# A two-layer decoder trunk on one core: the second layer in a hand-written TensorE order

## The chip, the cores and the metric

The kernel runs on one NeuronCore of one Trainium2 chip. The metric is the device time in microseconds of one execution. Engines go by the profile's names: PE (TensorE matmul), PEld (its weight loads), DVE (VectorE), ACT (ScalarE), POOL (GpSimd), SP (the queue that issues the DMAs).

## The reference

The input is 2048 tokens of width 1024. Layer 1 is gated linear attention, layer 2 dilated sliding-window attention in three (window, dilation) groups; each layer also has a small cross-attention into 256 memory tokens, a SiLU gate and an output projection. Layer 2, which the change concerns:

```
def dilated_mixer(h, w_in):
    for g, (window, dil) in enumerate(DIL_GROUPS):     # (128, 1), (512, 4), (2048, 16)
        qkv = (h @ w_in[:, base:base + 3 * 768]).reshape(B, T, 3, 6 heads, 128)
        q, k = partial_rope(qkv[:, :, 0]), partial_rope(qkv[:, :, 1])      # 32 of 128 dims turn
        o, lse = dilated_group(q, k, qkv[:, :, 2], window, dil)
    wts = softmax over the 3 groups of lse
    o = sum over groups of wts * outs
    ...                                                # q_mem and gate from the last columns
branch = concatenate([mix, mem_o]) * silu(gate)
x = x + branch @ w_out[i]
return rmsnorm(x, final_norm_w)
```

All of it is float32; the kernel splits each operand into a high and a low part and multiplies high by high, high by low and low by high.

## The kernel before, in words

**Helpers.** `mm3` (L178) is those three matmuls, at lines 179, 180 and 181, so nearly all TensorE work stands under three lines and is told apart by its tiles. `split_P` (L169) makes high (L172, ACT) and low (L173, POOL) halves of a probability tile and transposes both with one DMA (L174). `load_w` (L128) loads a block of weight columns, takes its norm (two squares on ACT, L114; a matmul with ones over the partitions, L118; a scale that is a power of two) and splits it (L138, L139). `mm_bank` (L730) hands out three PSUM banks in turn: two of `ps_mm`, one of `ps_x`. Scores use the two banks of `ps_g`, the value products the one bank of `ps_o`.

**Order.** The framework plans the order on every engine from an estimate of each instruction's time; PE too follows that plan. Every engine runs its own list in order.

**Layer 1** (up to about 932 us) ends with `a2_h2`, which writes `h2T`, the normed input of layer 2, transposed, in high and low halves (f16).

**Strassen stage** (L751 to L955). Thirteen sets of 256 columns of `w_in_b` (one of memory queries; three of gates, the gate of heads 4 and 5 not among them; nine of v, one for each pair of heads and each group) are multiplied by a one-level Strassen scheme: `sums` (L763) makes S1, S2 and S4 from quarters of `h2T` and overwrites one quarter with S3; `load_ws` (L788) makes seven combinations of a set's weights; `sblock` (L819) does seven products of 12 matmuls for half of the tokens, evacuated at L835, L840 and L842. Results go to DRAM: v transposed (`out_v`, `v_d`), gates after SiLU (`out_gate`, `sg_d`), queries (`qm_d`). Beside it runs the memory attention, one block of 128 tokens a step: `mem_a` (scores, softmax, transposing DMA) and, one step later, `mem_b` (values). At the end the overwritten quarter of `h2T` is loaded again from `a21_d`.

**Heads** (L957 to L1180). Nine units (pair of heads, group), two heads each. `proj_qk` (L985) makes q and k of one head, for four chunks of 512 tokens each: 24 matmuls, then the rope on that one tile: a shuffle (L1002, DVE), a product with the sines (L1003, POOL), one with the cosines (L1004, DVE, on the PSUM tile), their sum (L1005, DVE), and the high (L1007, ACT) and low (L1008, DVE) halves, which free the bank. `attend` (L1012) takes sixteen blocks of 128 queries two at a time: scores, mask and maximum (L1037), exponentials (L1048), `split_P`, value products, copy out (L1067, to `o_d`). `gate_prep` (L1086) and `gate_item` (L1121) later mix the three groups by their softmax weights (`fb`, read back from DRAM to all partitions) and multiply by the gate, into `br_d`; POOL has two of the products (L1135, L1140). Those of the first two pairs of heads run among later units; the last pair's stand after all heads, with the gate projection `gate_mm` of heads 4 and 5.

**Projection** (L1205 on). For sixteen blocks of 128 tokens `load_b` (L1209) loads and splits the branch (L1216, L1217); 2 x 24 matmuls of 512 columns in f32 parts follow (256-wide pieces in half of the last block), then the residual (L1244), the norm and the store.

Of the kernel before, what the change touches and what calls it, by code (L numbers as in the profile page):

```python
# [34 lines left out]
def trunk(ctx, tc, a, out):  # L35
# [259 lines left out]
    def silu(ps, n, inv, neg, dst, wk):  # L295
        e = tl(wk, [P, 512], F32, "e")
# [28 lines left out]
    v_d = {(hp, g, i): tl(dram, [P, 2, NB, P], F16, f"vd{hp}_{g}_{i}") for hp in range(3) for g in range(3)  # L325
           for i in range(2)}
    sg_d = {h: tl(dram, [P, T], F32, f"sgd{h}") for h in (0, 1, 2, 3, 6, 7)}
# [399 lines left out]

# [8 lines left out]

    def gdst(t, g, c):
# [7 lines left out]
    wp = c3.enter_context(pool("wpb", 4))  # L745
# [4 lines left out]

    with ExitStack() as cv:  # L751
        c4p = cv.enter_context(pool("c4p", 5))
        uv = cv.enter_context(pool("uv", 2))
        svp = cv.enter_context(pool("svp", 1))
        mc = cv.enter_context(pool("mc", 1))
        mk = cv.enter_context(pool("mk", 1))
        H = T // 2
        Ss = {n: tl(svp, [P, 2, 4, H], F16, n) for n in ("S1", "S2", "S4")}

# [3 lines left out]
        def sums(ts):  # L763
            n = ts.stop - ts.start

            def f32(i, k, eng):
                t = tl(c4p, [P, 4, n], F32, "c4")
                eng.tensor_tensor(out=t, in0=quad(i, k, 0, ts), in1=quad(i, k, 1, ts), op=ALU.add)
                return t

            def split(t, hi, lo, eng):
                A.activation(out=hi, in_=t, func=AF.Copy)
                eng.tensor_tensor(out=lo, in0=t, in1=hi, op=ALU.subtract)

            s = f32(1, 1, V)
            x21 = f32(1, 0, G)
            V.tensor_tensor(out=s, in0=s, in1=x21, op=ALU.add)
            split(s, Ss["S1"][:, 0, :, ts], Ss["S1"][:, 1, :, ts], V)
            x11 = f32(0, 0, G)
            V.tensor_tensor(out=s, in0=s, in1=x11, op=ALU.subtract)  # L780
            split(s, Ss["S2"][:, 0, :, ts], Ss["S2"][:, 1, :, ts], V)
            G.tensor_tensor(out=x21, in0=x11, in1=x21, op=ALU.subtract)
            split(x21, quad(1, 0, 0, ts), quad(1, 0, 1, ts), G)
            x12 = f32(0, 1, G)
            V.tensor_tensor(out=s, in0=x12, in1=s, op=ALU.subtract)
            split(s, Ss["S4"][:, 0, :, ts], Ss["S4"][:, 1, :, ts], V)

        def load_ws(c0, cps):  # L788
# [4 lines left out]
            wa = tl(wp, [P, 4, 2, 4, P], F16, "w")  # L793
            wb = tl(wp, [P, 3, 2, 4, P], F16, "w")
            junk = wa.rearrange("p f a k n -> p (f a k n)").bitcast(BF16)
            s, inv = norm_scale(raw, [junk[:, i * 1024:(i + 1) * 1024].rearrange("p (k n) -> p k n", n=256)
                                      for i in range(2)], cps)
            t13 = tl(c4p, [P, 2, 4, P], F32, "c4")
            t24 = tl(c4p, [P, 2, 4, P], F32, "c4")
            rq = raw.rearrange("p (q k) n -> p q k n", q=2)  # L800
            top = raw[:, 0:4, :].rearrange("p k (q n) -> p q k n", q=2)
            low = raw[:, 4:8, :].rearrange("p k (q n) -> p q k n", q=2)
            G.tensor_tensor(out=t13, in0=rq[:, :, :, P:2 * P], in1=top, op=ALU.subtract)
            G.tensor_tensor(out=t24[:, 0], in0=low[:, 1], in1=t13[:, 0], op=ALU.subtract)
            G.tensor_tensor(out=t24[:, 1], in0=low[:, 0], in1=t24[:, 0], op=ALU.subtract)
            A.activation(out=wb[:, 2, 0], in_=top[:, 0], func=AF.Copy, scale=s)
            A.activation(out=wa[:, 0:2, 0], in_=low, func=AF.Copy, scale=s)
            A.activation(out=wa[:, 2:4, 0], in_=t13, func=AF.Copy, scale=s)
            A.activation(out=wb[:, 0:2, 0], in_=t24, func=AF.Copy, scale=s)
            for src, dst in ((top[:, 0], wb[:, 2]), (low[:, 0], wa[:, 0]), (low[:, 1], wa[:, 1]),  # L810
                             (t13[:, 0], wa[:, 2]), (t13[:, 1], wa[:, 3]), (t24[:, 0], wb[:, 0]),
                             (t24[:, 1], wb[:, 1])):
                V.scalar_tensor_tensor(out=dst[:, 1], in0=src, scalar=s, in1=dst[:, 0], op0=ALU.mult,
                                       op1=ALU.subtract)
            V.tensor_tensor(out=inv, in0=inv, in1=invh1, op=ALU.mult)
            return dict(B21=wa[:, 0], B22=wa[:, 1], T1=wa[:, 2], T3=wa[:, 3], T2=wb[:, 0], T4=wb[:, 1],
                        B11=wb[:, 2]), inv

        def sblock(w, cc, sc):  # L819
            ts = slice(cc * 512, (cc + 1) * 512)  # L820
            aform = {"A11": quad(0, 0, 0, ts), "A12": quad(0, 1, 0, ts), "A22": quad(1, 1, 0, ts),
                     "S3": quad(1, 0, 0, ts)}
# [486 lines left out]
```

## Time and profile before

| | us |
|---|---|
| runs (median of 3; lowest, highest) | 2785.2; 2782.36, 2786.55 |
| the profiled execution: its time; its span | 2786.99; 2785.2 |
| busy in it: PE, PEld, DVE, ACT, POOL | 2553.5, 1679.4, 1697.5, 1205.8, 735.5 |
| mean granted TensorE clock | 0.967 |

The span runs from the first to the last instruction. A matmul's duration in the profile takes in its way through the array, so neighbours overlap and the busy share of PE reads high; the pace is read from one start to the next. The granted clock is 1 or 0.5 of full speed from moment to moment, and a window shows its mean.

### The profile page before, as it was taken

How to read it: one execution, taken by the hardware profiler on the slowest of the kernel's cores; microseconds unless marked ns; L12 is line 12 of the kernel's file. 1: busy time of each engine (PE TensorE's matmuls, PEld its weight loads, DVE VectorE, ACT ScalarE, POOL GpSimd, SP SyncE). 2: the span in 40 equal slices, each digit the busy share in tenths (PEclk: the TensorE clock that was granted, in tenths of full speed). 3: DMA queues.
4: the chain of work that ended last, by engine and by line, in shares of the span. 5: the costliest groups of instructions: out<-in, count | busy, mean ns of one | idle time of the engine just before them, and what ended most of it. 6: DMA issues, size and time to landing. Idle time of an engine off the chain costs nothing. (4 is left out here: it accounts for less than half of the span.)

```text
span 2785.2 us, 44184 instructions
## 1 busy us (share of the span) xinstructions
PE 2553.5 (92%) x16725; PEld 1679.4 (60%) x16725; DVE 1697.5 (61%) x3514; ACT 1205.8 (43%) x2635; POOL 735.5 (26%) x550
## 2 busy tenths in 40 slices
PE   7989999999998679989889999998899988996899
PEld 6879998888987334444444455554455544553677
DVE  6345444655566876455545767768777688765543
ACT  6356444544344355444445344434344333434122
POOL 0000000100002554334442233334543345331200
PEclk9999999999999789999999999999999999997899
DMA  6242113343333125576764434336843377425643
GB/s 205 85 137 72 58 53 113 103 101 88 97 103 92 55 67 140 126 160 138 162 144 107 150 85 99 98 82 168 215 134 91 83 197 199 107 77 144 220 161 118
DMA packets 522297, 336.62 MB, mean 121 GB/s; under 512 B 373170, under 2 KB 475236, under 8 KB 519780
## 3 DMA queue, kind: packets, MB, share of 16 engines
q1 hardware_dynamic: 522084, 333.80, 44.1%
q8 instruction: 131, 2.15, 0.3%
q14 instruction: 82, 0.67, 0.1%
HBM read 178.99 MB, written 89.57 MB: 96 GB/s over the span
## 5 line engine op out<-in xcount | busy, mean ns | idle before, releaser
L179 PE MATMUL ps_mm<-h2T,w 128*128 128x512 f16 x1128 | 435.5, 386 | 29.3 <-ACT c L840 12.7
L181 PE MATMUL ps_mm<-h2T,w 128*128 128x512 f16 x1128 | 435.2, 386 | 0.0
L180 PE MATMUL ps_mm<-h2T,w 128*128 128x512 f16 x1128 | 435.1, 386 | 0.0
L179 PE MATMUL ps_mm<-w,hT 128*128 128x256 f16 (+1 forms) x1408 | 388.3, 276 | 3.9 <-ACT v L488 1.9
L180 PE MATMUL ps_mm<-w,hT 128*128 128x256 f16 (+1 forms) x1408 | 387.1, 276 | 0.0
L181 PE MATMUL ps_mm<-w,hT 128*128 128x256 f16 (+1 forms) x1408 | 385.7, 275 | 0.4 <-DVE hT L382 0.4
L180 PEld LDWEIGHTS <-w 128*128 128x128 f16 x1944 | 192.3, 99 | 251.3 <-issue 55.0
L181 PEld LDWEIGHTS <-w 128*128 128x128 f16 x1944 | 192.6, 99 | 223.8 <-issue 21.3
L179 PEld LDWEIGHTS <-w 128*128 128x128 f16 x1944 | 192.7, 99 | 221.9 <-issue 16.6
L1003 POOL TENSOR_TENSOR sh<-sh,rope 32x512 f32<-32x512 f32 x144 | 183.7, 1276 | 328.4 <-DVE sh L1002 309.1
L173 POOL TENSOR_TENSOR stg<-mp,stg 128x512 f16<-128x512 f32 x16 | 18.6, 1161 | 838.9 <-DMA ogd<-og 460.2
L1048 ACT ACTIVATE pm<-pm,st,cols 128x256 f32<-128x256 f32 (+1 forms) x288 | 156.3, 544 | 189.5 <-DVE st L1042 187.0
L173 POOL TENSOR_TENSOR ph<-pm,ph 128x512 f16<-128x512 f32 (+2 forms) x144 | 139.6, 976 | 263.0 <-issue 144.4
L179 PE MATMUL ps_x<-h2T,w 128*128 128x512 f16 x504 | 192.2, 381 | 0.4 <-ACT c L842 0.4
L181 PE MATMUL ps_x<-h2T,w 128*128 128x512 f16 x504 | 192.5, 382 | 0.0
L180 PE MATMUL ps_x<-h2T,w 128*128 128x512 f16 x504 | 192.4, 382 | 0.0
L179 PEld LDWEIGHTS <-hT 128*128 128x128 f16 x1408 | 139.1, 99 | 24.4 <-issue 5.4
L180 PEld LDWEIGHTS <-hT 128*128 128x128 f16 x1408 | 139.0, 99 | 23.7 <-issue 5.3
L181 PEld LDWEIGHTS <-hT 128*128 128x128 f16 x1408 | 139.5, 99 | 18.2 <-DVE hT L382 0.7
L114 ACT ACTIVATE w<-stg 128x1024 bf16<-128x1024 f32 (+1 forms) x78 | 82.0, 1051 | 113.5 <-DMA stg<-in_w_in_b 70.2
L859 ACT ACTIVATE vh<-c 128x1024 f16<-128x1024 f32 x36 | 60.4, 1678 | 131.7 <-DMA vo<-vh 78.5
L179 PE MATMUL ps_g<-k,q 128*128 128x256 f16 (+1 forms) x288 | 70.2, 251 | 31.0 <-DVE mx L1037 26.6
(353 smaller groups left out, 5941.2 us busy)
## 6 DMA issues: line engine op xcount, KB each, us to landing
stg<-in_w_in_b SPq DMA_DIRECT2D x64, 512.0 KB
v<-vd SPq DMA_DIRECT2D x18, 1024.0 KB
od<-osb SPq DMA_DIRECT2D x72, 256.0 KB
og<-od SPq DMA_DIRECT2D x72, 256.0 KB
fb<-fd SPq DMA_DIRECT2D x24, 768.0 KB
x<-in_x SPq DMA_DIRECT2D x32, 512.0 KB
vd<-vo SPq DMA_DIRECT2D x48, 256.0 KB
hTd<-hT SPq DMA_DIRECT2D x16, 512.0 KB
```

The lines of the kernel that those rows point to most:

```text
L114: A.activation(out=junk[i], in_=hv, func=AF.Square, accum_out=rm[:, i:i + 1])
L173: G.tensor_tensor(out=lo, in0=src, in1=hi, op=ALU.subtract)
L179: PE.matmul(o, sh, mh, start=first, stop=False)
L180: PE.matmul(o, sh, ml, start=False, stop=False)
L181: PE.matmul(o, sl, mh, start=False, stop=last)
L859: A.activation(out=hi, in_=src, func=AF.Copy)
L1003: G.tensor_tensor(out=sw, in0=sw, in1=rs, op=ALU.mult)
L1048: A.activation(out=p_, in_=p_, func=AF.Exp, scale=sc, bias=st[:, j:j + 1], accum_out=st[:, 16 + j:17 + j])
```

## The change

Only layer 2 changes. PE follows the order in which the program is written (`manual_schedule` for PE alone); the other engines are planned as before.

- *Strassen stage.* The memory queries (192 matmuls) and the gate of head 4 (96) are done first, by ordinary projections, chunk by chunk, while `sums`, now in eight parts, are made. Twelve sets stay. Between the products of a block `side(i)` puts the next set's norm, combinations and splits, the memory attention (`mem_b` of one block after product 4, `mem_a` of the next after product 5) and what is left of the sums. `v_d` is laid out in chunks of whole rows.
- *Heads.* One head after another, each with groups 16, 4, 1. A stage is one chunk of q or of k (24 matmuls); stage s also holds the scores of step s − 10 and the value products of step s − 13, ahead of its projection. The rope is done for a chunk's q and k together after the second of them, with their 32 turning rows stacked in one tile. A head's weights are loaded, normed and split among the stages of the head before. The mixing is done per head, its loads some stages ahead of its products.
- *End.* The gate of head 5 is projected in eight halves beside the last head's scores and value products; that head's last group stays in SBUF (`osb`), as does its finished branch (`b5s`). `w_out` is split before. The projection takes the other seven 128-row blocks of the branch first (`f_main`) and head 5's last (`f_fin`); three such parts stand before the last value products are done. The first 512 output columns are done as two 256-wide pieces, for the weights lie in separate tiles.

```
+    def proj_t(w, c):
+        t = mm_bank()
+        for k in range(KT):
+            mm3(t, w[:, 0, k], w[:, 1, k], h2T[:, 0, k, cs], h2T[:, 1, k, cs], k == 0, k == KT - 1)
+        return t
...
+        cv.enter_context(tc.manual_schedule(engines={mybir.EngineType.PE}))
...
+        def sums(x):
+            ts = slice(x * P, (x + 1) * P)
+            x21 = f32q(1, 0, ts, G)
+            s = f32q(1, 1, ts, V)
+            V.tensor_tensor(out=s, in0=s, in1=x21, op=ALU.add)
+            split(s, Ss["S1"][:, 0, :, ts], Ss["S1"][:, 1, :, ts], V)
...
+        memq(2)
+        out_q(0, 0, proj_t(wq["w"][0], 0))
+        pair_norm(wg4, ps_g)
+        pair_split(wg4, 0)
...
+        out_q(0, 1, proj_t(wq["w"][1], 0))
+        gate4(2)
+        sums(0)
+        sums(1)
+        gate4(0)
+        sums(2)
+        memq(1)
+        set_norm(cur, ps_g)
+        sums(3)
...
+    def rope_pair(ts, c, g, dsts):
+        r0 = 64 * (c // 2)
+        rt = [rope[x][r0:r0 + 64, (c % 2) * 512:(c % 2 + 1) * 512] for x in range(2)]
+        X = tl(bk, [P, 512], F32, "rx")[r0:r0 + 64, :]
+        W = tl(bk, [P, 512], F32, "rw")[r0:r0 + 64, :]
+        for j in range(2):
+            A.activation(out=X[32 * j:32 * j + 32, :], in_=ts[j][0:32, :], func=AF.Copy)
+        V.stream_shuffle(W, X, SWAP)
+        G.tensor_tensor(out=W, in0=W, in1=rt[1], op=ALU.mult)
+        V.tensor_tensor(out=X, in0=X, in1=rt[0], op=ALU.mult)
+        for j in range(2):
+            V.tensor_tensor(out=ts[j][0:32, :], in0=X[32 * j:32 * j + 32, :], in1=W[32 * j:32 * j + 32, :], op=ALU.add)
+        for j in range(2):
+            hi = gdst(dsts[j][:, 0, :], g, c)
+            A.activation(out=hi, in_=perm(ts[j], g), func=AF.Copy, scale=SQ)
+            V.scalar_tensor_tensor(out=gdst(dsts[j][:, 1, :], g, c), in0=perm(ts[j], g), scalar=SQ, in1=hi,
+                                   op0=ALU.mult, op1=ALU.subtract)
...
+    for s in range(NS):                       # 18 heads x 8 stages
+        n, e = divmod(s, 8)
+        if s >= 10:
+            scores(s - 10)
+        if s >= 13:
+            pv(s - 13)
...
+        live[e % 2] = proj_t(d["w"][e % 2], e // 2)
+        if e % 2 == 1:
+            rope_pair([live[0], live[1]], e // 2, u[1], hds[n]["qk"])
+            wcur = wnext
+        if e == 2:
+            pair_norm(wcur, ps_tr)
+        elif 4 <= e < 4 + wcur["m"]:
+            pair_split(wcur, e - 4)
+        if e == 6:
+            hds[n]["v"] = load_v(n)
+        h, x = divmod(s - 35, 24)
+        if 0 <= h < 5:
+            step = 4 if h < 4 else 2
...
+            y, z = divmod(x - 5, step)
+            if 0 <= y < 4 and z == 0:
+                item_mix(*items.pop(y))
+            y, z = divmod(x - 3, step)
+            if 0 <= y < 4 and z == 0:
+                items[y] = (item_og(h, y), item_fb(h, y))
...
+    for x in range(14):
+        if x < 10:
+            scores(NS - 10 + x)
+        if x < 13:
+            pv(NS - 13 + x)
...
+        if x < 8:
+            gate_half(x)
...
+            P1, P2 = [(0, 256), (256, 256)], [(512, 512)]
...
+        if x in (8, 9):
+            fs[x - 8] = load_b(x - 8)
...
+        if x == 9:
+            f_main(fs[0], P1)
+        if x == 10:
+            f_main(fs[1], P1)
+        if x == 12:
+            f_main(fs[0], P2)
+            fs[2] = load_b(2)
```

More of the change, by code (lines that the diff above doesn't have):

```diff
@@ L807, in load_ws @@
[L807 to L814, printed above, removed]
@@ new lines, in trunk @@
+        out_q(0, 1, proj_t(wq["w"][1], 0))
[7 more added lines that the diff above has]
+        sums(3)
+        for x in ("T1", "T2", "T3", "T4"):
+            set_diff(cur, x)
+        gate4(1)
+        sums(4)
+        for x in range(4):
+            set_split(cur)
+        memq(3)
+        sums(5)
+        gate4(3)
+        for x in range(3):
+            set_split(cur)
+        late = [lambda x=x: sums(x) for x in (6, 7)]
```

931 lines of the change are left out of this document (545 added, 386 removed).

## The prediction

> **What bounds the kernel now.** I read the page's busy shares and clock row first, then windows cut at the program's stages, then PE's waits in each window, then the timeline for the pace of one matmul.
>
> ```profile
> PE 2553.5 (92%) x16725; PEld 1679.4 (60%) x16725; DVE 1697.5 (61%) x3514; ACT 1205.8 (43%) x2635; POOL 735.5 (26%) x550
> PEclk9999999999999789999999999999999999997899
> ```
>
> TensorE is busy for 92% of the span, no other engine for more than 61%; its clock row dips at the start of layer 2 and at its end. The columns of the windows are length, PE, PEld, DVE, ACT, POOL busy, granted clock, DMA share, GB/s:
>
> ```profile
> 0.00:886.00 886.00, 847.89 (x7441) 758.60 (x7442) 474.46 (x1094) 429.69 (x1003) 41.06 (x52) 0.99 0.33 100
> 886.00:932.00 46.00, 27.14 (x190) 21.20 (x188) 36.57 (x48) 18.28 (x34) 21.48 (x10) 0.78 0.33 104
> 932.00:1010.00 78.00, 45.52 (x162) 18.64 (x162) 70.93 (x48) 28.68 (x37) 58.16 (x23) 0.73 0.13 38
> 1010.00:1540.00 530.00, 486.25 (x2469) 229.01 (x2467) 282.88 (x441) 256.26 (x411) 205.10 (x130) 0.97 0.59 140
> 1540.00:2515.00 975.00, 924.43 (x5493) 484.33 (x5492) 708.07 (x1714) 394.67 (x978) 373.12 (x314) 0.99 0.49 125
> 2515.00:2612.00 97.00, 61.04 (x287) 37.28 (x283) 50.69 (x81) 35.88 (x69) 19.72 (x15) 0.79 0.60 181
> 2612.00:2779.00 167.00, 161.27 (x696) 130.39 (x696) 71.92 (x88) 41.35 (x100) 16.90 (x8) 0.96 0.46 157
> 2779.00:2785.20 6.20, 0.00 (x0) 0.00 (x0) 1.96 (x4) 1.00 (x4) 0.00 (x0) 0.78 0.23 85
> ```
>
> Row 1 is layer 1, unchanged. The others are: layer 1's last block, the start of layer 2, the Strassen products, the attention heads, gates and last combinations, the output projection, and the tail. PE stands idle there for 46 − 27.1 = 18.9, 32.5, 43.8, 50.6, 36.0 and 5.7 us, 187 us in all. While busy it also loses (1 − clock) × busy: 6 + 12.3 + 14.6 + 9.2 + 12.8 + 6.5 = 61 us. About 249 us of layer 2 are thus not matmul work at full pace, and only these can be won. Who ended the idle time, window by window:
>
> ```profile
> PE ps_g L118 <- DVE rb L116: 6.8, 1, 6.8
> PE ps_tr L166 <- DVE sg L692: 6.1, 1, 6.1
> ...
> PE ps_mm L179 <- ACT c L840: 10.0, 2, 6.5
> PE ps_g L258 <- DMA qmT<-qmd: 9.0, 1, 9.0
> ...
> PE ps_mm L179 <- DVE uv L835: 11.6, 3, 6.1
> PE ps_o L284 <- DMA mp<-mh: 11.4, 6, 5.3
> ...
> PE ps_g L179 <- DVE mx L1037: 23.3, 21, 3.6
> PE ps_o L179 <- DMA pt<-ph: 13.2, 18, 2.2
> ...
> PE ps_x L179 <- POOL fb L1135: 20.0, 1, 20.0
> PE ps_o L179 <- DMA pt<-ph: 6.1, 6, 2.2
> ```
>
> Nearly all are waits for a result that was asked for too soon: a score bank whose maximum isn't taken (L1037), probabilities not yet transposed (pt, mp), a combination not yet made. No engine is full, except VectorE in 932 to 1010 (70.9 of 78 us).
>
> **The change part by part.** The pace of matmuls, from starts (the first two pairs stand ten steps apart, the last pair are neighbours):
>
> ```profile
> 1603.09 0.38 PE L180 MATMUL ps_mm<-h2T,w 128*128 128x512 f16 x1
> ...
> 1605.25 0.38 PE L181 MATMUL ps_mm<-h2T,w 128*128 128x512 f16 x1
> ...
> 2759.67 0.39 PE L179 MATMUL ps_mm<-wh,w 128*128 128x512 f32 x1
> ...
> 2761.94 0.39 PE L180 MATMUL ps_mm<-wl,w 128*128 128x512 f32 x1
> ...
> 2775.41 0.28 PE L181 MATMUL ps_mm<-wh,w 128*128 128x256 f32 x1
> 2775.53 0.28 PE L179 MATMUL ps_mm<-wh,w 128*128 128x256 f32 x1
> ```
>
> A 512-wide f16 step is 2.16 / 10 = 0.216 us, an f32 one 2.27 / 10 = 0.227, a 256-wide f32 one 0.12.
>
> *Added matmuls.* The memory queries leave the Strassen form: 8 x 24 = 192 matmuls for 14 products x 12 = 168, so 24 x 0.216 = +5.2 us. The first half of the output columns is done in 256-wide pieces, for 16 blocks: 16 x 24 x (2 x 0.12 − 0.227) = +5.0 us. Gates of heads 4 and 5 keep their 192 matmuls and move. Together +10 us, all on PE's path.
>
> *Start (886 to 1010).* The 192 query matmuls and 96 of gate 4, 62 us at pace, now stand ahead of the first Strassen product and need only h2T and their weights. The cover for them is VectorE's: it must meanwhile make the sums 0 to 3 (eight 128x512 steps each). The nearest row, of twice the size:
>
> ```profile
> L773 DVE TENSOR_TENSOR S<-c,S x12: 1212/1944/3361, 934.9 to 1006.1; 128x1024 f16<-128x1024 f32 x12
> ```
>
> Half its median is 0.97: 4 x 8 x 0.97 = 31 us; sixteen query splits and eight gate steps at about 0.7 us (L1005's row, below) add 17, seven weight splits of the sums' size 7, three of twice that 6: 61 of 62 us. By the row's ends the sums alone are 20 or 54 us, so nothing or some 25 us stay uncovered; the row's smallest value is what an undisturbed step takes, and I take a value between, near the covered end: of 32.5 idle us I keep 6. Gate 4 brings per chunk 24 matmuls, two VectorE and three ACT steps and one store on SP, none of which anything waits for before the items. Layer 1's last block still ends in the same chain (rb, sg above): of 18.9 I keep 15 (bounds 5 and 25).
>
> *Strassen products.* Each memory PV now follows its scores by seven products (7 x 12 x 0.216 = 18 us) where the mp transposes made PE wait. Weight splits go two to a product, operand by operand; what is late next is the product's own evacuation (L835, three banks). Of 43.8 I keep 14 (bounds 3 and 44). The stores of v become whole 2 KB rows, the weight loads of the heads 512-byte rows; at a DMA share of 0.59 and 0.49 I cost both at nothing: they have a set or a head's eight stages (50 us) of cover. SP issues in order, so a late transpose holds up those loads; without cover each would cost its lateness.
>
> *Heads.* Scores now lag projections by ten stages, PV lags scores by three. The scores and PV of 144 stages are three lines each of these (the wide ones 0.108 us, half a 512 step, the narrow ones 0.054):
>
> ```profile
> L179 PE MATMUL ps_g<-k,q 128*128 128x256 f16 x162 | 44.3, 275 | 23.8 <-DVE mx L1037 19.6 <-ACT k L1007 3.6
> L179 PE MATMUL ps_g<-k,q 128*128 128x128 f16 x126 | 26.2, 220 | 7.2 <-DVE mx L1037 7.0
> L179 PE MATMUL ps_o<-pt,v 128*128 128x128 f16 x318 | 60.8, 221 | 21.7 <-DMA pt<-ph 19.3 <-DVE osb L1067 2.0
> L179 PE MATMUL ps_o<-pt,v 128*128 128x256 f16 x66 | 18.0, 273 | 0.0
> ```
>
> That is 3 x (228 x 0.108 + 444 x 0.054) / 144 = 1.0 us a stage beside 24 x 0.216 = 5.2 us of projection, so PV has 18 us of cover: the 23.3 and 13.2 us of waits above go. New is the pairing of q's and k's rope.
>
> ```profile
> L1002 DVE STREAM_SHUFFLE sh<-ps_mm x96: 715/723/746, 1541.1 to 2490.4; 32x512 f32<-32x512 f32 x96
> L1003 POOL TENSOR_TENSOR sh<-sh,rope x144: 1252/1262/1775, 1544.7 to 2498.0; 32x512 f32<-32x512 f32 x144
> L1004 DVE TENSOR_TENSOR ps_mm<-ps_mm,rope x96: 676/685/693, 1544.5 to 2491.2; 32x512 f32<-32x512 f32 x96
> L1005 DVE TENSOR_TENSOR ps_mm<-ps_mm,sh x96: 685/687/687, 1546.1 to 2492.6; 32x512 f32<-32x512 f32 x96
> L1007 ACT ACTIVATE q<-ps_mm x48: 569/588/597, 1548.2 to 2475.1; 128x512 f16<-128x512 f32 x48
> L1008 DVE SCALAR_TENSOR_TENSOR q<-ps_mm,q x48: 615/691/693, 1549.7 to 2476.4; 128x512 f16<-128x512 f32 x48
> ```
>
> Each of 72 pairs saves a shuffle and a cosine product (72 x 1.41 = 101 us of VectorE's 708), a GpSimd product (91 us of 373), and adds two ACT copies (at most L1007's 0.59 each: 85 us on 395). None of the three was the bound, so this gives PE nothing by itself. But q's bank is now held through k's projection. After that projection ends the chain is 0.59 (copy) + 0.72 + 1.26 + 2 x 0.69 (adds) + 0.69 (low part) = 4.6 us; the bank is wanted 5.2 + 2 x 1.0 = 7.2 us after, so 2.6 us are left for queueing. How long such queues get:
>
> ```profile
> ACT k L1007 <- DVE ps_mm L1005: 119.6, 31, 7.8
> POOL fb L1135 <- DMA fb<-fd: 27.0, 8, 5.7
> L1144 DVE TENSOR_TENSOR fb<-fb x24: 677/692/1641, 1921.0 to 2662.4; 128x512 f32<-128x512 f32 x24
> ```
>
> 31 waits of ACT for VectorE's rope add sum to 119.6 us, one of 7.8: most pairs fit, some don't. At 0.25 us a pair this is 18 us; with 12 us of other waits I keep 30 of 50.6 (bounds 8, and 72 x 1.4 = 101). Twenty gate items are spread at four stages each with fb loaded two stages (12 us) ahead; the four of head 4 come into the heads: six DMAs each on SP, whose two-stage lead covers them, and about 3.5 us each on VectorE and GpSimd, hidden while VectorE is at (708 − 101 + 14) / 955 = 65%. Without that cover they cost 4 x 3.5 = 14 us.
>
> *End.* The 20.0 us wait for the last items goes: 96 gate matmuls (20.7 us) now run beside the last scores and PV, head 5 skips its o and br round trips, and three parts of the projection start on seven blocks. New: the first branch load needs h2T's space, freed by the last gate matmul; load, copy and subtract (some 3 to 8 us) meet only four score and PV groups, 2.6 us. Of 36.0 I keep 9 (bounds 4 and 25). *Projection:* 3 of 5.7 stay; the tail of 6.2 us stays.
>
> **Sum.** Idle kept: 15 + 6 + 14 + 30 + 9 + 3 = 77, so 110 us go. Half-rate loss shrinks in the same proportion, 61 to 25: 36 us go. 110 + 36 − 10 = 136. The profiled execution took 2787.0 us, 1.8 more than its span of 2785.2, which is also the runs' median; 2785 − 136 gives about 2648 for the median.
>
> **A rule against it.** VectorE's L1004 reads one operand from PSUM and stays within 0.693 us beside GpSimd; L1144 reads two from SBUF and reaches 1.641. In the new rope the cosine product reads X and the table, both SBUF, just as GpSimd multiplies W. If one stands still for the other, each chain grows by 0.69 to 5.3 us. The Trainium skill, SBUF — State Buffer, section Who interferes with whom, says that a VectorE instruction with two SBUF inputs contends with a GpSimd instruction that reads SBUF, one waiting for the whole of the other; L1144's spread agrees. By that rule the sum would be 50 us higher if no slack were left, unchanged if 2 us remain.
>
> **Rivals.**
> - *Every gap goes* (lags of three to ten stages cover all queues): keeps 5 + 2 + 3 + 8 + 4 + 2 = 24, loss 8: 163 + 53 − 10 = 206, 2579 us. Against: the 7.8 us queue.
> - *The rope holds the banks:* each pair late by 0.69 us more, 72 x 0.69 = 50: 2698 us. For it: L1144; against: 101 us less VectorE work.
> - *The fixed order does nothing in the middle* (products and heads keep their idle time): the start and end alone give 29 + 27 + 3 and some 20 of clock, less 10: 2716 us.
> - *Slower than before:* GpSimd stands in order at an item's fb, and behind it the rope and the splitting of probabilities, so PE stops. Twenty items must each lose 136 / 20 = 6.8 us. With two stages, 12.4 us, of lead fb would have to land after 19 us; its longest overhang here was 5.7. Then 2785 or more.
>
> **How the numbers follow.** My forecast 0.55 (its own range 2605 to 2690), every gap 0.15, rope 0.18, middle unchanged 0.05, slower 0.07. The range 2590 to 2735 leaves out half of "every gap" and all of "slower", under 2 in 10. A measurement here tells 0.2% (5.6 us) from no change: faster 0.91, same 0.02, slower 0.07.
>
> **What would show it.** Right: heads' window near 925 us with clock 0.99 or more; no wait of PE for L1037's maximum or pt; the start without a dip to 0.73; no 20 us wait after the gates; 256-wide f32 steps of 0.12. Wrong: PE waiting every second stage for the low part of q, or for rb of a weight norm; GpSimd idle on fb for over 6 us; VectorE above 90% in the heads.

## The result, and the profile after

The changed kernel takes 2749.4 us (median of 4 runs, 2743.2 to 2756.2), the kernel before 2785.9: a ratio of 0.9869 [0.9838, 0.9899]. It is 36 us faster where 136 were forecast, and lies 14 us above the range. The profiled execution took 2743.2 us, its span is 2741.4. The page's busy row and clock row:

```profile
PE 2546.4 (93%) x17137; PEld 1699.6 (62%) x17137; DVE 1642.0 (60%) x3483; ACT 1311.6 (48%) x2921; POOL 649.2 (24%) x513
...
PEclk9999999999999989999999999899998999998899
```

The busy shares look almost as before. The windows by stage (columns as before: length, PE, PEld, DVE, ACT, POOL, granted clock, DMA share, GB/s) show that the time has moved:

```profile
886.00:932.00 46.00, 43.64 (x272) 26.65 (x270) 22.06 (x41) 20.63 (x39) 4.52 (x4) 1.00 0.37 117
932.00:1036.00 104.00, 68.26 (x289) 29.14 (x287) 100.15 (x117) 47.94 (x81) 62.32 (x41) 0.87 0.18 53
1036.00:1553.00 517.00, 512.59 (x2680) 246.41 (x2679) 297.66 (x539) 290.43 (x560) 215.72 (x162) 1.00 0.59 150
1553.00:2520.00 967.00, 875.90 (x5151) 459.09 (x5149) 641.15 (x1507) 459.87 (x1087) 303.84 (x243) 0.95 0.51 131
2520.00:2573.00 53.00, 35.17 (x219) 29.27 (x218) 36.22 (x82) 18.50 (x38) 13.85 (x8) 0.79 0.62 161
2573.00:2735.00 162.00, 161.56 (x1054) 147.56 (x1052) 66.76 (x97) 42.54 (x108) 7.00 (x4) 0.99 0.43 143
```

Idle time of PE is length less busy; the loss at half clock is (1 − clock) × busy, as in the prediction (us):

| stage | idle before | idle forecast | idle after | loss before | loss after |
|---|---|---|---|---|---|
| layer 1's last block | 18.9 | 15 | 2.4 | 6.0 | 0 |
| start of layer 2 | 32.5 | 6 | 35.7 | 12.3 | 8.9 |
| Strassen products | 43.8 | 14 | 4.4 | 14.6 | 0 |
| heads | 50.6 | 30 | 91.1 | 9.2 | 43.8 |
| end | 36.0 | 9 | 17.8 | 12.8 | 7.4 |
| projection | 5.7 | 3 | 0.4 | 6.5 | 1.6 |

Outside the heads, idle time and loss together fell from 189 to 79 us, a gain of 110. The heads went from 60 to 135 us and gave 75 of it back. So most of the expected gain was made, and two thirds of it were lost again in one stage; that, and the start, are what the experiments are about.

PE's waits in the heads (us in total, times, longest), 1553 to 2520:

```profile
PE ps_mm L179 <- DVE q L1142: 64.1, 16, 7.4
PE ps_x L179 <- DVE q L1142: 21.0, 10, 4.1
```

The waits for scores are gone and those for transposed probabilities nearly so (3.3 us), as forecast. In their place a projection waits for its bank until VectorE has made the low part of q, the step of the paired rope (L1133 to L1142) that frees this bank. The timeline shows the chain of one pair that nothing disturbs (start, duration, engine, line). At 1616.07 ScalarE begins the copy out of k's bank, right at the end of k's projection:

```profile
1616.07 0.58 ACT L1133 ACTIVATE rx<-ps_x 32x512 f32<-32x512 f32 x1 [2.60 <-PE ps_x L181]
...
1616.78 0.42 DVE L1173 CUSTOM_DVE_ANT_0 pm<-ps_g,mw 128x256 f32<-128x256 f32 x1
...
1617.24 0.72 DVE L1134 STREAM_SHUFFLE rw<-rx 64x512 f32<-64x512 f32 x1
...
1618.00 0.69 DVE L1211 COPY osb<-ps_o 128x512 f32<-128x512 f32 x1
1618.11 1.27 POOL L1135 TENSOR_TENSOR rw<-rw,rope 64x512 f32<-64x512 f32 x1 [3.42 <-DVE rw L1134]
...
1618.72 0.68 DVE L1177 TENSOR_SCALAR st<-mx,cols 128x2 f32<-128x2 f32 x1
1619.44 0.69 DVE L1136 TENSOR_TENSOR rx<-rx,rope 64x512 f32<-64x512 f32 x1
...
1620.23 0.69 DVE L1138 TENSOR_TENSOR ps_mm<-rx,rw 32x512 f32<-32x512 f32 x1
...
1621.13 0.58 ACT L1141 ACTIVATE q<-ps_mm 128x512 f16<-128x512 f32 x1
...
1621.74 0.69 DVE L1142 SCALAR_TENSOR_TENSOR q<-ps_mm,q 128x512 f16<-128x512 f32 x1
...
1623.36 0.38 PE L179 MATMUL ps_mm<-h2T,w 128*128 128x512 f16 x1
```

q's bank is free at 1622.43, 6.4 us after the start, and wanted at 1623.36, 7.3 us after. Only 0.9 us are to spare (the median over the pairs between 1560 and 2460 is 6.4 us of chain, and nearly all undisturbed ones from 1600 to 1860 have 0.9 to 1.3 to spare).

One small step matters here. L1177 scales the maxima of two blocks of queries. It has two columns and takes 0.23 us in the median where GpSimd is idle; here it takes 0.68 and ends as GpSimd's product ends. It does so in 36 of the 38 places in the heads where the two met, 0.02 to 0.03 us behind the product. The cosine product (L1136), which doesn't need GpSimd's, stands behind it in the queue. So the 1.27 and the 0.69 us come one after the other.

Now a pair in which an item, the gate mixing of a head and chunk (L1286 to L1300), gets into the queues:

```profile
1741.39 0.68 DVE L1136 TENSOR_TENSOR rx<-rx,rope 64x512 f32<-64x512 f32 x1
...
1744.23 1.03 DVE L1291 TENSOR_TENSOR fb<-og,fb 128x512 f32<-128x512 f32 x1 [2.16 <-DMA fb<-fd]
1744.30 2.04 POOL L1289 TENSOR_TENSOR fb<-og,fb 128x512 f32<-128x512 f32 x1 [2.85 <-DMA fb<-fd]
...
1745.18 1.71 DVE L1138 TENSOR_TENSOR ps_mm<-rx,rw 32x512 f32<-32x512 f32 x1
1746.30 1.95 POOL L1294 TENSOR_TENSOR fb<-og,fb 128x512 f32<-128x512 f32 x1
...
1746.92 1.89 DVE L1138 TENSOR_TENSOR ps_x<-rx,rw 32x512 f32<-32x512 f32 x1
...
1750.04 0.68 DVE L1142 SCALAR_TENSOR_TENSOR q<-ps_mm,q 128x512 f16<-128x512 f32 x1
...
1750.77 0.58 PE L179 MATMUL ps_mm<-h2T,w 128*128 128x512 f16 x1 [5.46 <-DVE q L1142]
```

VectorE has the cosine product done at 1742.07, then stands 2.16 us in order at the item's first product, whose factors (fb) haven't landed. The rope's adds come behind it and take 1.71 and 1.89 us instead of 0.69 while GpSimd does the item's other products. PE stands for 5.46 us, and its next matmul takes 0.58 us instead of 0.38: the clock has been halved. Such gaps stand in groups of four, at 1712, 1730, 1745 and 1766 us and again every 173 to 176 us, which is one head with its three groups (24 stages), at the four items of each head.

### The profile page after: what moved, and what is told of

Its sections match the earlier page's. It is cut to its first block, busy times and chain, and to the rows that moved or that the text cites. A ratio compares the mean times of both kernels' runs of the same rounds, so it can differ in the third digit from the quotient of the medians.

```text
span 2741.4 us, 45032 instructions
## 1 busy us (share of the span) xinstructions
PE 2546.4 (93%) x17137; PEld 1699.6 (62%) x17137; DVE 1642.0 (60%) x3483; ACT 1311.6 (48%) x2921; POOL 649.2 (24%) x513
## 4 chain that ended last, share of the span: by engine, by line
PE 69%; DVE 12%; DMA 9%; issue 4%; ACT 3%; POOL 2%; SPq 1%; DVEq 0%; POOLq 0%; ACTq 0%
PE ps_mm L179 14%; PE ps_mm L180 13%; PE ps_mm L181 13%; PE ps_x L179 5%; PE ps_x L181 5%; PE ps_x L180 5%; DMA fb<-fd 3%; DMA stg<-in_w_in_b 2%; PE ps_tr L166 1%; PE ps_o L181 1%; PE ps_o L180 1%; PE ps_o L179 1%; DMA pt<-ph 1%; DVE ps_mm L1138 1%; DVE fb L1297 1%
## 5 line engine op out<-in xcount | busy, mean ns | idle before, releaser
L173 POOL TENSOR_TENSOR ph<-pm,ph 128x512 f16<-128x512 f32 (+2 forms) x144 | 154.8, 1075 | 481.7 <-ACT ph L172 369.4
L179 PE MATMUL ps_x<-h2T,w 128*128 128x512 f16 x552 | 211.9, 384 | 38.9 <-DVE q L1142 21.7
L181 PE MATMUL ps_x<-h2T,w 128*128 128x512 f16 x552 | 211.7, 383 | 0.0
L180 PE MATMUL ps_x<-h2T,w 128*128 128x512 f16 x552 | 211.7, 383 | 0.0
L1173 DVE CUSTOM_DVE_ANT_0 pm<-ps_g,mw 128x256 f32<-128x256 f32 (+1 forms) x288 | 93.5, 360 | 153.1 <-PE ps_g L181 152.1
L1135 POOL TENSOR_TENSOR rw<-rw,rope 64x512 f32<-64x512 f32 x72 | 96.2, 1336 | 228.6 <-DVE rw L1134 210.8
L181 PEld LDWEIGHTS <-hT 128*128 128x128 f16 x1408 | 139.2, 99 | 17.8 <-DVE hT L382 0.7
L1133 ACT ACTIVATE rx<-ps_mm 32x512 f32<-32x512 f32 x96 | 56.1, 584 | 113.2 <-PE ps_mm L181 109.6
L179 PE MATMUL ps_o<-pt,v 128*128 128x128 f16 (+1 forms) x384 | 75.7, 229 | 9.7 <-DVE rw L1211 3.7
```

Source lines behind the costliest of these rows:

```text
L173: G.tensor_tensor(out=lo, in0=src, in1=hi, op=ALU.subtract)
L179: PE.matmul(o, sh, mh, start=first, stop=False)
L180: PE.matmul(o, sh, ml, start=False, stop=False)
L181: PE.matmul(o, sl, mh, start=False, stop=last)
L1133: A.activation(out=X[32 * j:32 * j + 32, :], in_=ts[j][0:32, :], func=AF.Copy)
L1135: G.tensor_tensor(out=W, in0=W, in1=rt[1], op=ALU.mult)
```

## The experiments

From this profile the theory was: (a) the items' steps stand in VectorE's queue ahead of the rope, (b) the paired rope has little to spare. The rivals: the pairing alone holds the banks; VectorE is full; the planned order as such is bad. Each time is the median of 4 runs, each ratio is to the kernel before (2785 to 2789 us), with a 95% interval. VectorE's queue is ordered ahead of time by costs and due times, and then runs in order; TensorE's is in the order written.

### Which part costs: items, pairing, order, sums

**n1: no mixing products for heads 0 to 4.**

```
 def item_mix(it, fb, osb=None):
     h, c, sg, og = it
+    if osb is None:
+        SY.dma_start(br_d[c][:, :, h, :], sg...); return sg
```

> The changed kernel without the five products and sums that mix the three groups in the twenty items of heads 0 to 4 (their loads of og, fb and the gate stay, and the gate alone is stored). In the changed kernel the heads' window is 967 us with 91 us idle at a clock of 0.95, and PE waits 85 us for the low part of q. Theory 'items between the rope's steps' (the planned order puts item steps, which wait for fb, ahead of the rope's adds on VectorE and of its sine product on GpSimd): those waits go, the heads' window falls to 850 to 880 us, the whole to about 2640 to 2660. Rival 'pairing' (q's bank held through k's projection stalls PE by itself): the waits stay, over 2720. Rival 'transfers' (the item loads' traffic delays weights or transposes): the waits stay too, since the loads stay.

Measured: 2690.1 us, 0.9647 [0.9628, 0.9666], so the items cost 59 us. It did not come down to the time that the items' theory gave: PE still waits 30 us for q's low part (1560 to 2450, 12 and 5 times, where it was 78 in 25). The items' loads stayed, so their traffic isn't what the 59 us are.

**n5: the rope per tile,** on the bank itself, right after its own projection, as in the kernel before; TensorE's order is unchanged.

```
-        if e % 2 == 1:
-            rope_pair([live[0], live[1]], e // 2, u[1], hds[n]["qk"])
+        rope_one(live[e % 2], e // 2, u[1], hds[n]["qk"][e % 2], e % 2)
```

> The changed kernel with the rope of the kernel before: one tile at a time, on PSUM, right after its own projection, in the same stages and the same TensorE order. It adds 144 - 72 shuffles and cosine products on VectorE (101 us) and as many sine products on GpSimd (91 us), and frees q's bank one stage sooner. Rival 'pairing': the waits for q's low part go and the whole falls to 2640 to 2670. Theory 'items between the rope's steps': the items' steps still cut in, but there is a stage more of room for q: part of the 85 us goes, 2690 to 2720, unless VectorE's extra 101 us takes it back.

Measured: 2698.6 us, 0.968 [0.9666, 0.9695]: 51 us better than paired. The edit does two things that no run parts: it frees q's bank a stage sooner, and the cosine product reads PSUM again, so that it has one SBUF input only. PE no longer waits for q, but at the items now for the copy of the attention output out of its one bank, again behind the item in VectorE's queue (1560 to 2450):

```profile
PE ps_o L179 <- DVE osb L1225: 56.8, 14, 7.6
```

**n3: VectorE and GpSimd too in program order** through the 144 stages.

```
+    order.enter_context(tc.manual_schedule(engines={DVE, Pool}))
     for s in range(NS):
```

> The changed kernel with VectorE and GpSimd too in the order of the program during the 144 stages, so that an item's steps come after a whole rope and before the next one; same work. Theory 'items between the rope's steps': nearly all of the 85 us of PE's waits for q's low part go, 2650 to 2680. Rival 'port' (VectorE steps with two SBUF operands stand still while GpSimd's item products read SBUF, wherever they are placed): half of the waits stay, about 2700. Rival 'pairing': no change, 2735 to 2755. A plain order may also make VectorE wait in the rope (for the sine product, 72 x 1.3 us of its own time, not of PE's).

Measured: 2849.2 us, 1.0219 [1.0202, 1.0236], a miss by 170 us. VectorE's and PE's waits from 1560 to 2450 say why:

```profile
DVE rw L1134 <- ACT rx L1133: 218.0, 37, 8.5
```

```profile
PE ps_o L179 <- DVE osb L1211: 93.0, 42, 6.5
PE ps_tr L776 <- DVE rb L774: 42.7, 14, 4.9
```

The program writes a stage's rope right behind its projection, so VectorE waits for the projection's end, and what stands behind (the copy of the attention output, the norms' sums) comes late to PE. The order made by costs is 100 us better than this one.

**n6: the start's sums wholly on VectorE,** none on GpSimd.

```
-            x21 = f32q(1, 0, ts, G)
+            x21 = f32q(1, 0, ts, V)
...
-            split(x21, quad(1, 0, 0, ts), quad(1, 0, 1, ts), G)
+            split(x21, quad(1, 0, 0, ts), quad(1, 0, 1, ts), V)
```

> The changed kernel with the sums S1 to S4 and their differences wholly on VectorE (GpSimd's four steps of each of the eight sums moved: 28 steps of 128x512, at 0.68 us each some 19 us more for VectorE). In the changed kernel the start (932 to 1036 us) has 36 us idle, VectorE busy for 100 of 104 us, with steps of 0.68 us stretched to 1.5 to 1.8 beside GpSimd. Theory 'port': the stretches go, VectorE gets through the same work sooner, the start's idle time falls to 10 to 20 us: total 10 to 25 us less. Rival 'too much work for VectorE': the start grows by up to 19 us.

Measured: 2753.3 us, 0.9879 [0.9864, 0.9894], no change, where one theory had 10 to 25 us less. The start's window has 27 more VectorE instructions than the changed kernel's in 5 us less busy time, and GpSimd has little left:

```profile
932.00:1036.00 104.00, 71.54 (x305) 30.77 (x304) 95.45 (x144) 49.57 (x82) 18.48 (x12) 0.89 0.17 55
```

What VectorE took over, it saved in stretching. One of the sums' subtractions (minimum, median, maximum in ns), in the changed kernel and here:

```profile
L842 DVE TENSOR_TENSOR c<-c,c x8: 676/1500/1782, 941.5 to 1009.1; 128x512 f32<-128x512 f32 x8
```

```profile
L842 DVE TENSOR_TENSOR c<-c,c x8: 682/687/1751, 951.6 to 1014.3; 128x512 f32<-128x512 f32 x8
```

### Items without pairing, the load, the start, an order by hand

**n7: rope per tile and no mixing products** (n5 and n1 together).

> The rope per tile as in the kernel before, and the mixing products of heads 0 to 4 left out as well (their loads stay; the gate alone is stored). In the version with the rope per tile every gap of TensorE between 1720 and 2460 us stands at an item: 63 us of gaps, and 61 us at half clock behind them, which lose 30. If the items are all that is left there, the time falls by some 90 from 2698.6, to 2600-2625. If the paired rope was not needed for the loss and something else feeds the gaps (VectorE full, the norms, the statistics), gaps appear in other places and it stays above 2650.

Measured: 2645.2 us, 0.9493 [0.9477, 0.9509], 20 above its band but below 2650. With n1 and n5 this makes a square: items cost 53 us with the rope per tile and 59 paired; pairing costs 45 without items and 51 with them. Here the two add up; neither explains the other away. (In later runs, with the items held apart, pairing cost 12 us, n15 against n16, and 78, n17 against n19: what it costs depends on what else is late.)

**n8: n5 with fb in two buffers.**

```
-        fb = tl(gk, [P, 3, 16, 32], F32, "fb")
+        fb = tl(fbp, [P, 3, 16, 32], F32, "fb")   # fbp: 2 buffers; pm 2, ph 3 instead of 4
```

> The rope per tile, all items in place, but the factors' tile fb in two buffers (paid for by two buffers fewer of pm and one fewer of ph), so that its 768 KB can be under way while the item before is still at work. If what stops TensorE is VectorE waiting in order for fb's load, 2-4 us an item: 2615-2640. If it is the item's own work on VectorE and GpSimd, 7 us in one lump, that is late: 2680-2700, no change. If the order of VectorE, which is planned ahead with a shorter load than the real one, only moves the items forward by as much: also near 2698.

Measured: 2689.8 us, 0.9654 [0.9639, 0.9669], 9 us less, where the runs of either kernel spread over 7 us. VectorE's waits for fb fell from 21.5 us in 14 to 7.5 in 5 (1560 to 2450), yet PE's wait is nearly all still there:

```profile
PE ps_o L179 <- DVE osb L1228: 49.5, 17, 6.7
```

So the late load is a small part. But the run changed a second thing: with a free buffer the planned order put the four items of a head only 12 to 20 VectorE instructions apart, instead of 22. That gave the next idea: an item is 4.8 us of VectorE (1.02 + 1.99 + 0.69 + 1.05 us, medians of the changed kernel), the program spreads the four over sixteen stages, some 100 us, and the order of the changed kernel packs them into 52 us (1717.4 to 1769.7 in the first head).

**n9: the start with the first of three sums alone;** the other two are left out, and the products read the first in their place.

```
-            V.tensor_tensor(out=s, in0=s, in1=x11, op=ALU.subtract)
-            split(s, Ss["S2"]..., V)
-            x12 = f32q(0, 1, ts, V)
-            V.tensor_tensor(out=s, in0=x12, in1=s, op=ALU.subtract)
-            split(s, Ss["S4"]..., V)
```

> The changed kernel, but only the first of the three sums of each of the eight pieces is made; the products that want the other two read the first (the output is not the reference's). 40 VectorE steps of 0.68 us fewer, 27 us, and 16 ScalarE copies. If the start is bound by VectorE, which was busy 100 of the 104 us from 932 to 1036: those 27 us and a part of the 15 us that half clock costs there, 2705-2725. If it is bound by the chain of one gate (projection, gate steps, bank) or by the order alone: 2740-2750.

Measured: 2716.4 us, 0.9745 [0.9729, 0.9761]: 33 us less, as VectorE's bound has it.

```profile
932.00:1036.00 104.00, 90.94 (x418) 41.00 (x417) 80.57 (x96) 53.21 (x90) 71.51 (x48) 0.98 0.34 93
```

PE does 418 matmuls there instead of 289, at 0.98 of the clock. The start is bound by VectorE's work on the sums.

**n10 and n11: n5 with VectorE's and GpSimd's order by hand.** In both a stage finishes the rope of the stage before, and an item's steps are dealt over three stages. n11 differs in what stands first (shortened; a minus is n10's order, a plus n11's, and lines without a sign stand in both):

```
 for s in range(NS):
+    if e == 3: norm_r(wnext)                 # n11: row sums ahead of the stage
     late = rope_a(*late)                     # shuffle, GpSimd's product, cosine
-    scores(s - 10); pv(s - 13)               # n10
-    rope_b(*late)                            # n10: add, high part, low part
+    pv(s - 13)                               # n11
+    late = rope_b(*late)                     # n11: add, high part
+    scores(s - 10)
+    rope_c(*late)                            # n11: low part
     ...
     parts[y][z]()                            # a third of an item
```

> The rope per tile, and VectorE's and GpSimd's order in the 144 stages written by hand too: a stage has first the shuffle and the cosine product of the stage before, then the maxima, the copy of the attention output, then the add and the low part of the stage before, and last a part of an item; an item's five VectorE steps are dealt over three stages, its loads two stages ahead, the weight norms over three stages. If the items' wait and the order are the cause, nearly all gaps between 1550 and 2460 go: 2600-2635. If order by hand costs by its in-order waits, as program order did with the paired rope (2849): above 2700.

Measured: 2835.4 us, 1.017 [1.015, 1.019]. PE waited for the norms' row sums, behind the rope in VectorE's queue (1553 to 2520):

```profile
PE ps_tr L802 <- DVE rb L800: 85.7, 15, 7.8
```

> The second order by hand, with the rope per tile. In the first (2835), VectorE waited 1.2-1.9 us in each stage for ScalarE's high part, TensorE waited 86 us in all for the norms' row sums that stood behind the rope in VectorE's queue, and 40 us of VectorE went on the statistics' transpose behind a projection. Now a stage has: shuffle, cosine, copy of the attention output, add, the maxima, low part; the row sums go ahead of the stage, the transpose ahead of the scores, an item's steps in the three stages after its load is due. If these in-order waits were the cause: 2640-2670 (without the mixing products it was 2645). If a fixed order of VectorE costs in itself, because it can't take what is ready: above 2720.

Measured: 2765.0 us, 0.9918 [0.9901, 0.9935], 70 us better than n10 and still 66 worse than the order by costs. Now VectorE waited for GpSimd's rope product, which stood behind the probabilities' low part in GpSimd's queue (1560 to 2450):

```profile
DVE ps_mm L1196 <- POOL rw L1191: 81.6, 31, 7.3
DVE ps_x L1196 <- POOL rw L1191: 75.6, 20, 12.4
```

The second order by hand took away one in-order wait and showed the next. Three fixed orders of VectorE and GpSimd thus lost 100 (n3), 137 (n10) and 66 us (n11) to the order by costs. That a better one can't be written is not shown.

### The copy of the attention output on ScalarE

**n13: in the changed kernel; n14: in n8.**

```
-            V.tensor_copy(osb, ob)
+            A.activation(out=osb, in_=ob, func=AF.Copy)
```

> The changed kernel with one step moved: the copy of the attention output out of PSUM (0.69 us, every second stage) goes from VectorE to ScalarE, which is busy 419 of 890 us in the heads. In a pair that nothing disturbs, q's bank comes free 6.4 us after k's projection and is wanted after 7.4; the copy stands in this chain in VectorE's queue. If these 1.0 us of slack are what lets each item's lump reach TensorE, 1.7 us of slack save up to 0.7 us at some 25 places with half clock behind them: 2715-2740. If the copy isn't on the chain, or ScalarE's queue takes as long: 2745-2755. If VectorE's load as such is the bound in the heads: 48 us less work, near 2710.

Measured: 2748.5 us, 0.9855 [0.984, 0.987], no change, as in its second case. In the timeline above the copy runs beside GpSimd's 1.27 us product, so it was not on the chain. Without it the cosine product moves beside that product, and one of the two is held up: in 32 of the 72 pairs GpSimd's takes 1.70 to 1.88 us, in the other 40 the cosine product takes 1.1 to 1.7 instead of 0.69. And the item's wait stays where it was:

```profile
1754.99 1.01 DVE L1291 TENSOR_TENSOR fb<-og,fb 128x512 f32<-128x512 f32 x1 [5.07 <-DMA fb<-fd]
1755.92 0.68 DVE L1142 SCALAR_TENSOR_TENSOR q<-ps_mm,q 128x512 f16<-128x512 f32 x1
...
1756.65 0.58 PE L179 MATMUL ps_mm<-h2T,w 128*128 128x512 f16 x1 [7.93 <-DVE q L1142]
```

Here q's low part, ready to run, stands behind a wait of 5.07 us for fb, and PE with it for 7.93 us.

> The rope per tile, fb in two buffers, and the copy of the attention output on ScalarE. With the rope per tile TensorE's waits at the items are all for this copy (49.5 us, 17 times), which stands behind the item in VectorE's queue, while the rope has three banks and the maxima ten stages. If that is the place where an item reaches TensorE: 2640-2660. If the rope's banks are next in line at once, or ScalarE is behind by as much: 2675-2695.

Measured: 2687.8 us, 0.9642 [0.9626, 0.9658], 2 less than n8: no gain, as in its second case. PE now waits 24.9 us for the copy, on ScalarE, and 15.6 for the rope of q and k.

### Items held back to their own stage

**n15: n8 and a hold** for each item; **n16: paired rope, two fb buffers and the hold; n18: the changed kernel and the hold alone; n17 and n19: n15 and n16 with the copy on ScalarE.** The hold is two small ScalarE steps. The first makes 1.0 from that stage's maxima, the second passes three columns of fb through it, so neither VectorE nor GpSimd can be given the item earlier:

```
+    def hold(fb):
+        g1 = tl(sp, [P, 1], F32, "g1")
+        A.activation(out=g1, in_=last_st[0], func=AF.Copy, scale=0.0, bias=1.0)
+        A.activation(out=fb[:, :, 0, 0:1], in_=fb[:, :, 0, 0:1], func=AF.Copy, scale=g1)
...
             if 0 <= y < 4 and z == 0:
+                hold(items[y][1])
                 item_mix(*items.pop(y))
```

> The rope per tile and fb in two buffers (2690), and each item held back to its own stage: two ScalarE steps of one to three columns, the second of which passes a piece of fb through a factor of 1.0 that is made from that stage's maxima. VectorE's order then has the items of a head 43 to 53 instructions apart instead of 12 to 20; every step and load is the same. If the loss at the items is that four of them, 27 us of VectorE, are packed into some 45 us that have 31 us of other work already: 2645-2665, as without the products (2645) and a little more. If each single item stops TensorE whatever its distance: 2685-2700.

Measured: 2684.7 us, 0.9626 [0.9602, 0.9649]: 5 us less than n8, as if each item stopped TensorE whatever its distance. The four items of the first head take 15.0 us of VectorE in n8, not the 27 expected, so there was less to spread out. PE still waits 35.8 us in 16 places for the copy of the attention output.

> The changed kernel with its paired rope, fb in two buffers and the same hold. Packing theory: towards the paired rope without the products (2690), with something for single items, since a pair has only 1.0 us to spare: 2695-2720. If the wait for fb's load was not the matter and each item's 5 us of VectorE go through to TensorE (20 x 4 us and half clock): 2740-2750, no change.

Measured: 2696.7 us, 0.9669 [0.9646, 0.9691]: 53 us less than the changed kernel.

> As the first of these, with the copy of the attention output on ScalarE as well. If single items still reach TensorE through this copy: 5-15 us below the first. If nothing is left there: equal within 5 us.

Measured: 2640.5 us, 0.9471 [0.9451, 0.9491]: 44 us less than n15, far more than expected, and the best version. PE's waits for the copy went from 35.8 us in 16 places to 17.4 in 7 (1560 to 2450); with the half clock behind such waits that is a good part of the 44, and the rest is not traced here. Its heads, of which I take 1540 to 2395, have 12.6 us idle at full clock:

```profile
1540.00:2395.00 855.00, 842.37 (x5128) 448.74 (x5127) 667.29 (x1628) 400.90 (x1040) 369.26 (x307) 1.00 0.56 141
```

> The changed kernel with the hold alone: each item of heads 0 to 4 kept back to its own stage by two small ScalarE steps, fb in its one buffer. If the packing of the items is the cause, and not the buffer: 2690-2710, as with two buffers (2697). If the second buffer carried the gain: above 2730.

Measured: 2695.1 us, 0.9681 [0.9658, 0.9704]. The hold alone, with one fb buffer, brings 54 us. The items of a head now stand 38 to 49 VectorE instructions apart, where they stood 19 to 28 apart. The hold moves a second thing: fb now goes through ScalarE first, so VectorE hardly waits for its load any more (1560 to 2450, first the changed kernel, then n18):

```profile
DVE fb L1291 <- DMA fb<-fd: 21.4, 14, 3.7
```

```profile
DVE fb L1299 <- ACT fb L1150: 3.3, 6, 0.9
```

No run parts the distance of the items from this wait with the paired rope. With the rope per tile, taking most of the wait away while the items stood even closer brought 9 us (n8). The same window of both, first the changed kernel, then n18:

```profile
1560.00:2450.00 890.00, 809.57 (x4749) 423.27 (x4747) 590.70 (x1388) 419.41 (x995) 279.87 (x225) 0.96 0.50 128
```

```profile
1560.00:2450.00 890.00, 841.14 (x5037) 444.57 (x5036) 625.22 (x1470) 448.27 (x1091) 285.56 (x238) 0.98 0.56 137
```

In the same 890 us PE does 288 more matmuls, VectorE does 82 more instructions and is busier: it was not full before. PE's waits for q's low part there:

```profile
PE ps_mm L179 <- DVE q L1142: 33.4, 20, 3.4
PE ps_x L179 <- DVE q L1142: 10.7, 10, 2.1
```

They were 56.7 us in 15 and 21.0 in 10: more of them, none above 3.4 us.

> The paired rope, fb in two buffers, the hold, and the copy of the attention output on ScalarE: beside the same with the rope per tile (2640) it has only the pairing more. If the pairing is harmless once items come one by one: 2640-2655. If q's bank, wanted 7.4 us after k's projection, stays the tightest wait (19 and 12 waits for q's low part, 46 us, in the run without this copy's move): 2675-2695.

Measured: 2718.4 us, 0.9769 [0.9747, 0.9792], 22 us more than n16. The pairing is not harmless: beside n17 it costs 78 us. VectorE now waits for GpSimd's rope product, and PE for q (1560 to 2450):

```profile
DVE ps_mm L1141 <- POOL rw L1138: 26.8, 23, 1.2
```

```profile
PE ps_mm L179 <- DVE q L1145: 44.6, 20, 6.1
PE ps_x L179 <- DVE q L1145: 19.4, 10, 3.0
```

The median pair frees q's bank 6.75 us after k's projection, 0.3 later than without the copy's move: the copy now stands in ScalarE's queue, where the pair has four steps of its own. The cosine product also moves beside GpSimd's, as in n13. How much of the 22 us each makes stays open.

## Why the prediction was wrong, point by point

- **The step that failed first is the rope chain: "the chain is ... 4.6 us; the bank is wanted ... 7.2 us after, so 2.6 us are left for queueing".** When the bank is wanted was right (7.3). The chain is 6.4 us. I added durations of some of the rope's own steps and left out the maxima ahead of the shuffle (0.6), the cosine product, which VectorE does only after GpSimd's product (0.7), q's high part on ScalarE ahead of the low part (0.6), and the hand-overs from engine to engine (0.55 in all). I counted two adds where one lies on the path (0.7 too much). With 0.9 us to spare instead of 2.6, 0.25 us a pair was the wrong size: pairing costs 45 us (n1 against n7) to 51 (changed kernel against n5), not 18. One of the signs of being wrong thus came true, PE waiting for the low part of q; the other two did not (GpSimd waited for fb 3.2 us at the longest, VectorE was busy 66%).
- **The items were taken as hidden behind a VectorE that is busy 65% of the time.** It was busy 66% in the heads (641 of 967 us), so the share was right and told nothing. Four items, 4.8 us each and not 3.5, were queued in 52 us and each of the 20 stopped PE, for 2.0 to 7.4 us. Held apart, with the same steps and the two small ones of the hold, they cost 54 us less (n18), of which the shorter wait for fb is a part that is not measured by itself. I took the program's spacing, four stages, for the queue's; nothing in the trace of before had shown the order that VectorE would be given. "fb loaded two stages (12 us) ahead" fell with it: VectorE waited 21.4 us for fb in 14 places.
- **Half clock.** I let its loss shrink with idle time, 61 to 25 us. It stayed at 62, since gaps of 2 to 8 us in the heads took the place of others: 9.2 us there became 43.8.
- **Start: 6 us idle forecast, 35.7 measured.** I laid the 61 us of VectorE's work for sums 0 to 3 against 62 us of matmuls. The queue also held the other four sums (the last step of the eight ends at 1028.4 us), the next weights and v's low parts, and stretched steps (1.50 us in the median for a subtraction that takes 0.68, L842 above): VectorE was busy 100 of 104 us. PE's largest waits are for VectorE steps behind sums:

```profile
PE ps_x L179 <- DVE c L1003: 15.0, 2, 13.4
PE ps_x L179 <- DVE c L899: 13.5, 1, 13.5
```

- **Right:** PV's and the scores' waits go; the Strassen stage keeps 4.4 us of idle time, better than 14; layer 1's last block 2.4, since the query matmuls fill its bubbles; the projection 0.4; the 20.0 us wait for the last items is gone. The end kept 17.8 instead of 9, 10.3 of it waiting for a branch's split into high and low part (3.9, 3.8 and 2.6).
- **Matmul work:** forecast 10 us more, measured at full clock 9 us less (1644 to 1635 us over the six windows). Some records are missing and ends are modelled, so I draw nothing from it.
- **The rivals.** "The rope holds the banks" had the right place and a part of the cause. The cosine product itself takes 0.69 us in an undisturbed pair, but it comes after GpSimd's, behind a step that is held up until that ends: 0.7 of the 1.8 us by which the chain is longer than I added up. The rest is other steps and hand-overs, and the items come on top. The slower rival had the mechanism of the items, an engine in order at fb with the rope behind it. Both engines stood there (1560 to 2450: VectorE 21.4 us in 14 places, GpSimd 32.6 in 19); in the pair shown the adds stood behind VectorE's wait. It cost 54 us in 20 items, 2.7 each, not 6.8. "Every gap goes" asked for heads nearly without gaps; n17 has them, with another rope and other item places.
- **The rule of the Trainium skill** (SBUF — State Buffer, Who interferes with whom) agrees with the trace where two SBUF inputs met GpSimd: the adds above took 1.71 and 1.89 us for 0.69, in n13 one of the two products was held up in every pair, and n6 shows that what is moved off GpSimd comes back as shorter VectorE steps.

## What to carry to other kernels

Slack on a bank is not the sum of a chain's durations against the time till it is wanted: walk the queues of the engines that the chain passes, and count what stands ahead in each. When one engine's order is fixed by hand and the others are ordered ahead of time, look where that order puts long off-path work, above all steps that wait for a load; tying such work to its own stage cost two small steps and brought 54 us. A busy share of 66% says nothing of four lumps of 5 us in a row, and a move that gains nothing while they are there (n14, 2 us) can gain 44 us once they are apart (n17).

## What the runs showed of the hardware

How long a gap of PE must be before the clock is halved could be read from the traces of ten versions (the changed kernel, n5, n8 and n13 to n19), from one matmul's start to the next, less its usual pace. I took gaps between 1560 and 2450 us that stand alone (10 us on either side without another over 0.4 us). None of 80 under 2.0 us was followed by a half-clock stretch, 7 of 20 from 2.0 to 2.5 us were, 16 of 19 from 2.5 to 3.4 us, and all 50 above. The stretches last 3.4, 6.8 or 10.2 us, the longest only after gaps above 6.5 us. A gap of 3 us thus costs its 3 us and as a rule another 1.7. The Trainium skill, TensorE: Matmul & The Clock Gate, section What's actually happening, names an idle window of about 3.4 us. The length of the stretches agrees with it, but here gaps of 2.0 to 3.4 us were enough in 23 of 39 cases.
